# Moving the query and key blocks of an encoder step's projection from the RWKV preparation to behind five iterations of its state chain

## The chip, the cores and the metric

The kernel runs on one core of one Trainium2 chip. The metric is the device time of one execution in microseconds (us); lower is better. The medians are taken over several executions of the same program; a profiled execution of the same program gives the rows that are read below.

## What is computed

One inference step of a one-layer streaming encoder, in float32, on 1024 prompt tokens and 8 sample streams with 16 new tokens each (1152 tokens, 9 tiles of 128, width 1024):

```
x = x + 0.5 * SwiGLU_1(RMSNorm(x))
P = RMSNorm(x) @ w_in                 # RWKV columns: r, k, v (512 each) and 256 low-rank; then q, k, v (512 each)
mix = concat(RWKV7(P_rwkv), BandAttn(P_att)) @ w_out
x = x + mix
x = x + 0.5 * SwiGLU_2(RMSNorm(x))
y = RMSNorm_final(x)
```

RWKV7 keeps a 64 x 64 state for each of 8 heads and carries it through the tokens one after the other: decay, removal along a normed key direction, addition of a key-value product, then a read by the query, a group norm and a gate. BandAttn is softmax attention of 8 heads over a band of 512 + 64 earlier positions with a relative bias; the streams use their caches. The outputs are y, the last projected rows, the states and the new key and value rows.

## The kernel before

The weights and the activations of a projection are split into a float32r part and a rest, and a product is made in three passes (`_mm_cols`, L211 to L220): 8 chunks of the inner dimension times 3 passes, for each of 3 groups of 384 tokens, so 72 matmuls for a column block of 128. `_load_w` (L159) loads a block's weights over the SP queue into `raw`, and ScalarE and GpSimd split them into `spl`; in the middle part there are 2 `raw` and 3 `spl` buffers (L1141).

The first feed-forward half and the last one, each a long run of dense matmuls, lie before and behind the part that the change touches. That part goes as follows.

**Projection and preparation** (`_project`, L282). `shifted(c)` projects one RWKV column block (`ps_p`) into a buffer `pt` behind the row before it. There are 4 `pt` buffers. For each of 4 head pairs p, three blocks are projected (r, k, v), and `_rwkv_prepare` (L480) makes what the state chain needs for the pair, in 5 groups of 256 tokens and three stages: token shift, decays and key norms (`_prepare_tokens`, reads `pt` at L273 and L274), scaled keys and queries (`_prepare_chunks`), and products, transposes and gates, which go to DRAM over the SP queue (`_prepare_products`). Most of its operations are small ones on VectorE, ScalarE and GpSimd, with a few matmuls between them. Behind each pair L337 places two blocks of `_attention_in` (L396): the queries and the keys of that attention head pair. Such a block has 72 matmuls (`ps_qk`, 3 x 24), its evictions on ScalarE (L414) and VectorE (L415, L421), for keys a transpose (`ps_ko`, L429) and its eviction (L432), one weight load on the SP queue and 7 (queries) or 10 (keys) stores on ScalarE's queue. Behind pairs 1 and 2 and behind the whole, `_invert` (L665) inverts the chunks' triangular matrices on VectorE, 62 operations a call, four calls.

**Chain and values.** `_rwkv` (L860) is a generator of 10 iterations of 4 chunks each; `_rwkv_run` (L752) makes one. A chunk is a sequence in which every step needs the one before: 16 matmuls (L771), a copy on VectorE, 16 matmuls (L776), four copies, 16 matmuls (L780), two multiplications on VectorE, beside 16 matmuls for the output (L784). An iteration has 192 matmuls that write `ps_c`. Its operands are loaded one iteration ahead over the SP queue (`_rwkv_load`, two buffers each), and the group norm of an iteration (`_rwkv_post`, L823) runs inside the next one, partly on GpSimd. L1153 places three iterations, then `_attention_inputs` (L355): the blocks of `QK[NQK:]` (none, as `NQK` is 8), the key caches, and the values, 18 tiles of 24 matmuls with 256 columns (`ps_av`, 432 in all).

**Attention.** Only then are the projection's pools closed and attention's buffers opened in their place (L1156, L1164). `_attention` (L1008) yields 74 steps for 72 units (pair, tile, head): scores (`ps_s`, L941), exponentials, transposes (`ps_pt`, L980, 256 in all), products with the values (`ps_o`, L994). Its loads are issued on GpSimd's queue (`k.aq`, L1167). L1169 to L1171 place one chain iteration and six units by turns, then the rest of the units. The output projection comes behind all of it.

**What sets the order.** No order is written out by hand. A scheduler at build time goes through the operations with the program order as priority and its own estimate of their durations: on each engine it places the earliest operation whose operands and buffers are ready, and when that one isn't ready, a later one that is. So matmuls that need nothing from the preparation or the chain end up in their gaps, as far as buffers allow. The order that comes out is fixed in each engine's queue, and a queue is worked off in order.

```
QK = [(p, kind) for p in range(NPAIR) for kind in range(2)]   # L55
NQK = 8                                                       # L56
...
        for q in QK[NQK * p // NPAIR:NQK * (p + 1) // NPAIR]: # L337
            _attention_in(k, w, *q)
```

Of the kernel before, what the change touches and what calls it, by code (L numbers as in the profile page):

```python
# [19 lines left out]
NPT = 8                 # prompt token tiles  # L20
NT = 9                  # token tiles, the last one holds the sample group
T = NT * P
TG = 384                # tokens of a moving operand
DFF = 2816
NF = DFF // P
NB, NQ = 8, 16          # sample streams and their new tokens
HD = 64
NPAIR = 4               # head pairs of each mixer
NH = 2 * NPAIR
NRC = 14                # 128-wide column chunks of the RWKV part of w_in  # L30
L = 32                  # RWKV chunk
NG = 5                  # groups of 8 RWKV chunks, the last one is the sample group
NCK = 8 * NG            # RWKV chunks of a head
# [4 lines left out]
# rows of the table of small vectors  # L38
# [8 lines left out]
# ---------------------------------------------------------------- constants  # L47
# [8 lines left out]
NQK = 8  # L56
# [18 lines left out]
def _vectors(k, parts, queue):  # L75
    """Columns of the table of small vectors."""
# [29 lines left out]
def _bias_tables(k, a):  # L106
    """Per head pair, in DRAM: the relative biases of a prompt tile's two near key tiles and of
    the sample group's keys, less the table's first entry (the bias of all far keys), with the
    masks added."""
# [16 lines left out]
    for p in range(NPAIR):  # L126
# [10 lines left out]
        # row q, column c of the skewed view: entry 127 + c - q  # L137
# [14 lines left out]
# ---------------------------------------------------------------- weights, norms  # L152
# [6 lines left out]
def _load_w(k, src, shape, rearr, **kw):  # L159
    """A weight block of 1024 words a partition as its float32r part and the rest."""  # L160
    raw = k.w.tile([P] + shape, F32, tag="raw", bufs=k.nraw, name="raw")
    k.wq.dma_start(raw, src.rearrange(rearr, **kw) if rearr else src)
    pool, nspl = k.spl
    d = pool.tile([P, 2] + shape, F32R, tag="spl", bufs=nspl, name="spl")
    _split(k, d, raw)
    return d
# [6 lines left out]
def _rms(k, i, xn):  # L173
    """The inverse root mean square of token tile i; xn is scratch."""
# [13 lines left out]
def _norm_t(k, v0):  # L188
    """By steps: k.xg[g] <- split of the transposed, normed token group g."""
# [21 lines left out]
def _mm_cols(k, ps, w, g):  # L211
    """ps [128 columns, 384 tokens] <- w^T x of token group g, in three passes."""
# [10 lines left out]
# ---------------------------------------------------------------- SwiGLU  # L223
# [44 lines left out]
# ---------------------------------------------------------------- projection  # L268

def _shift_mix(k, out, cur, prev, c):  # L270
    """out <- prev mu + cur (1 - mu) for column chunk c."""
# [5 lines left out]
def _sample_view(t):  # L277
    """The sample columns of a shifted chunk: [stream, shifted-in row and new tokens]."""
    return t[:, 1025:SPAN].rearrange("p (b l) -> p b l", l=NQ + 1)


def _project(k, a):  # L282
# [5 lines left out]
    # token-shift states, transposed to [column, stream, chunk]  # L288
# [8 lines left out]
    def shifted(c):  # L297
        """Column chunk c of the projection behind the row before: prompt, then the streams."""
# [18 lines left out]
    # the low-rank inputs: the gate's sigmoid, and tanh(decay part) | rate part  # L317
# [37 lines left out]
def _attention_inputs(k, a):  # L355
    """Queries and keys, then values, to DRAM and the caches."""
# [8 lines left out]
    # attention values, token-major  # L365
# [30 lines left out]
def _attention_in(k, w, p, kind):  # L396
    """Queries (scaled, kind 0) or keys of attention head pair p, feature-major and split, to
    DRAM; the keys also go to the caches, token-major."""
# [7 lines left out]
    # part, head, feature  # L406
# [33 lines left out]
# ---------------------------------------------------------------- RWKV  # L440

def _prepare_constants(k, a):
# [5 lines left out]
    # masks of the products: strict s < t for the keys, s <= t for the queries  # L448
# [22 lines left out]
    # the decays' and the rates' low-rank weights, each over zeros for the other's inputs  # L471
# [8 lines left out]
def _rwkv_prepare(k, p, low, pr, pk, pv):  # L480
    """What the chunks of head pair p need besides the running state, to DRAM, in three stages a
    group; a group's stage comes after the stage before of the next group."""
# [6 lines left out]
def _prepare_more(k):  # L489
    """The later stages of the groups that are begun."""  # L490
# [11 lines left out]
def _prepare_tokens(k, p, g, low, pr, pk, pv):  # L502
    """Token shift, decays and the norms of the key directions."""
# [3 lines left out]
    q = _K()  # L507
# [10 lines left out]
    # token shift of r, k, v  # L518
# [15 lines left out]
    # decay: running sum of the sigmoids inside a chunk, and its exponentials  # L534
# [17 lines left out]
    # key direction, normed inside the head  # L552
# [11 lines left out]
def _prepare_chunks(k, q):  # L564
    """The scaled keys and queries of the chunks."""
# [20 lines left out]
    # keys and queries scaled by the decay since the chunk's start  # L586
# [17 lines left out]
def _prepare_products(k, q):  # L604
    """Products of keys with keys and queries inside the chunks, masked; the time-major keys and
    values, the gates and the offsets."""
# [27 lines left out]
    # time-major keys  # L634
# [7 lines left out]
    # time-major values  # L642
# [7 lines left out]
    # gates with the group norm's weight; its offset and the values' bonus, gated  # L650
# [14 lines left out]
def _invert(k, *parts):  # L665
    """To DRAM: (I - A)^-1 by substitution, an inverse a partition, of every chunk of the parts: a
    head pair and its groups."""
# [20 lines left out]
def _chunk_constants(k, a):  # L688
# [5 lines left out]
    # state weights: the identity over the chunk's keys  # L694
# [6 lines left out]
def _rwkv_load(k, i):  # L701
    """The operands of four chunks, half i % 2 of group i // 2.

    Of every chunk and head, by turns:
# [532 lines left out]
```

## Time and profile before

| | us |
|---|---|
| median of 3 runs | 2640.08 |
| lowest and highest run | 2636.32, 2643.09 |
| span of the profiled execution (first to last instruction) | 2638.9 |

The profiled execution is told by its span alone; what lies around the span has no row. The span is 1.2 us under the median of the runs, so a change of the span is added to the median as it is.

In the profile a row of a stretch gives, for a window of the span, the busy time of each engine in it with the number of its instructions, the granted TensorE clock as a share of full speed, the share of time in which the DMA engines were busy and the rate. A busy TensorE is not one at its peak: the ends of matmuls are modelled, so the times of neighbours overlap, and the spacing of starts tells more than the durations. The profile cuts the part that the change touches at these points: 943.5, where the first pair's projection is done; 1029.4, 1120.4 and 1211.4, the same for the other three pairs; 1292.9, the chain's first matmul; 1357.8, the end of the values; 1386.9, the first scores; 1607.0, the chain's end; 1685.5, the end of attention.

### The profile page before, as it was taken

Reading aid. Unit: us, or ns where it says so; the run is one execution under the profiler, and the core shown is the slowest. Engines: PE = TensorE matmul, PEld = TensorE weight load, DVE = VectorE, ACT = ScalarE, POOL = GpSimd, SP = SyncE. Lnnn points to the kernel's source line nnn. Section 1 sums busy time; section 2 is a strip of 40 time slices with the busy share of each in tenths; the row PEclk is TensorE's granted clock in tenths of the full one; section 3 lists DMA queues with packets and bytes.
Section 4 is the critical chain, followed back from the end, with each engine's and each line's share of the span. In section 5 each row is a group of like instructions: output and inputs, shape, how many; then the busy total and the mean of one; then the engine's idle time right before and its main releaser. Section 6 shows DMA issues by size and latency. Waiting matters only on the chain.

```text
span 2638.9 us, 39574 instructions
## 1 busy us (share of the span) xinstructions
PE 2534.1 (96%) x16344; PEld 2296.9 (87%) x16344; DVE 1206.3 (46%) x2460; ACT 646.9 (25%) x1294; POOL 762.5 (29%) x686
## 2 busy tenths in 40 slices
PE   8999999999999899999987898899999999999998
PEld 8999999999998799989865666689999999999997
DVE  4442344234426344585846766523442344234425
ACT  5111111111111444344113334504111111111112
POOL 3222222222221334344133423103222222222231
PEclk9999999999999899999987789899999999999999
DMA  5311111111111243354669856301111111111111
GB/s 185 113 41 40 40 49 40 41 40 49 41 32 72 65 135 114 113 165 143 171 155 234 198 122 183 123 0 57 48 40 41 40 49 41 41 40 49 40 32 73
DMA packets 247797, 217.39 MB, mean 82 GB/s; under 512 B 54016, under 2 KB 218496, under 8 KB 247232
## 3 DMA queue, kind: packets, MB, share of 16 engines
q1 hardware_dynamic: 214252, 167.74, 21.9%
q0 software_dynamic: 7648, 25.43, 4.0%
q10 hardware_dynamic: 25716, 21.68, 2.7%
q8 instruction: 129, 2.11, 0.3%
q14 instruction: 52, 0.43, 0.1%
HBM read 155.35 MB, written 59.45 MB: 81 GB/s over the span
## 4 chain that ended last, share of the span: by engine, by line
PE 49%; DVE 5%; issue 2%; DMA 1%; POOL 1%; SPq 1%; ACT 1%; POOLq 0%; ACTq 0%; DVEq 0%
PE pg L220 3%; PE pg L218 3%; PE pg L219 3%; PE pu L220 3%; PE pd L256 3%; PE pu L218 3%; PE pu L219 3%; PE pd L258 3%; PE pd L257 3%; PE ps_o L994 2%; PE ps_wo L1067 1%; PE ps_wo L1065 1%; PE ps_wo L1066 1%; PE ps_s L941 1%; PE ps_pt L980 1%
## 5 line engine op out<-in xcount | busy, mean ns | idle before, releaser
L156 POOL TENSOR_TENSOR spl<-raw,spl 128x1024 fp32r<-128x1024 f32 x166 | 399.4, 2407 | 794.0 <-ACT spl L155 793.9
L260 DVE TENSOR_TENSOR x<-pd,x 128x512 f32<-128x512 f32 x774 | 527.4, 691 | 7.0 <-PE pd L258 2.9
L244 DVE SCALAR_TENSOR_TENSOR hf<-pu,sl 128x384 f32<-128x384 f32 x132 | 73.6, 558 | 963.5 <-PE pu L220 948.4
L218 PE MATMUL pg<-xg,spl 128*128 128x384 f32 x1056 | 356.2, 337 | 0.0
L220 PE MATMUL pg<-xg,spl 128*128 128x384 f32 x1056 | 355.4, 337 | 0.0
L219 PE MATMUL pg<-xg,spl 128*128 128x384 f32 x1056 | 355.3, 336 | 0.0
L220 PE MATMUL pu<-xg,spl 128*128 128x384 f32 x1056 | 355.0, 336 | 0.0
L218 PE MATMUL pu<-xg,spl 128*128 128x384 f32 x1056 | 354.9, 336 | 0.0
L219 PE MATMUL pu<-xg,spl 128*128 128x384 f32 x1056 | 354.9, 336 | 0.0
L155 ACT ACTIVATE spl<-raw 128x1024 fp32r<-128x1024 f32 x166 | 174.9, 1057 | 634.6 <-PE pd L258 421.8
L256 PE MATMUL pd<-spl,h 128*128 128x512 f32 x792 | 310.6, 392 | 0.0
L258 PE MATMUL pd<-spl,h 128*128 128x512 f32 x792 | 310.4, 392 | 0.0
L257 PE MATMUL pd<-spl,h 128*128 128x512 f32 x792 | 310.4, 392 | 0.0
L247 POOL TENSOR_TENSOR h<-hf,h 128x384 fp32r<-128x384 f32 x132 | 133.9, 1014 | 591.0 <-ACT h L246 577.3
L218 PEld LDWEIGHTS pg<-xg,spl 128*128 128x128 f32 x1056 | 198.5, 188 | 1.7
L219 PEld LDWEIGHTS pg<-xg,spl 128*128 128x128 f32 x1056 | 198.5, 188 | 1.5
L220 PEld LDWEIGHTS pg<-xg,spl 128*128 128x128 f32 x1056 | 198.3, 188 | 0.0
L220 PEld LDWEIGHTS pu<-xg,spl 128*128 128x128 f32 x1056 | 198.2, 188 | 0.0
L218 PEld LDWEIGHTS pu<-xg,spl 128*128 128x128 f32 x1056 | 198.2, 188 | 0.0
L219 PEld LDWEIGHTS pu<-xg,spl 128*128 128x128 f32 x1056 | 198.2, 188 | 0.0
L258 PEld LDWEIGHTS pd<-spl,h 128*128 128x128 f32 x792 | 148.6, 188 | 33.7
L257 PEld LDWEIGHTS pd<-spl,h 128*128 128x128 f32 x792 | 148.5, 188 | 31.9
(227 smaller groups left out, 3710.3 us busy)
## 6 DMA issues: line engine op xcount, KB each, us to landing
raw<-in_w_ff_gate_dram SPq DMA_DIRECT2D x44, 512.0 KB
raw<-in_w_ff_up_dram SPq DMA_DIRECT2D x44, 512.0 KB
raw<-in_w_ff_down_dram SPq DMA_DIRECT2D x44, 512.0 KB
raw<-in_w_in_dram SPq DMA_DIRECT2D x26, 512.0 KB
q<-qk POOLq DMA_DIRECT2D x24, 384.0 KB, 7.4
ard<-ar SPq DMA_DIRECT2D x20, 256.0 KB
grd<-gram SPq DMA_DIRECT2D x20, 256.0 KB
wsd<-tb SPq DMA_DIRECT2D x20, 256.0 KB
```

Source lines behind the costliest of these rows:

```text
L155: k.nc.scalar.activation(dst[:, 0], raw, AF.Copy)
L156: k.nc.gpsimd.tensor_tensor(dst[:, 1], raw, dst[:, 0].bitcast(F32), ALU.subtract)
L218: mm(ps, w[:, 0, c], hi[:, c], start=c == 0, stop=False)
L219: mm(ps, w[:, 0, c], lo[:, c], start=False, stop=False)
L220: mm(ps, w[:, 1, c], hi[:, c], start=False, stop=c == KC - 1)
L244: nc.vector.scalar_tensor_tensor(hf, pu[:, :TG], 0.5, sl, ALU.mult, ALU.mult)
L247: nc.gpsimd.tensor_tensor(h[:, 1, s], hf, h[:, 0, s].bitcast(F32), ALU.subtract)
L256: mm(ps, ph[:, 0, a], pd[:, 0, b], start=j == 0, stop=False)
L257: mm(ps, ph[:, 0, a], pd[:, 1, b], start=False, stop=False)
L258: mm(ps, ph[:, 1, a], pd[:, 0, b], start=False, stop=j == len(pend) - 1)
L260: nc.vector.tensor_tensor(xs, ps, xs, ALU.add)
L994: mm(po[hs, :P], q.v[:, u.j0 + j, hs], u.pt[:, j * P:(j + 1) * P], start=j == 0, stop=j == nj - 1)
```

## The change

`NQK` becomes 0, so the loop at L337 places no block, and all eight blocks of queries and keys are placed by `_attention_inputs`, pair by pair, ahead of the values. Five chain iterations instead of three are placed ahead of `_attention_inputs`, and eight units instead of six behind each of the five iterations that are left. No operation, buffer or queue is added or removed. (The diff also strips comments and docstrings, with no effect.)

```diff
-NQK = 8
+NQK = 0
...
         chain = _rwkv(k, a)
-        for _ in range(3):
+        for _ in range(5):
             next(chain)
         _attention_inputs(k, a)
         s_xg.close()
...
             for _ in chain:
-                for _ in range(6):
+                for _ in range(8):
                     next(units, None)
```

## Rows read from the trace of the kernel before

**Rows 1.** the profile's page: span, TensorE's busy time, granted clock in 40 slices

```profile
span 2638.9 us, 39574 instructions
PE 2534.1 (96%) x16344; PEld 2296.9 (87%) x16344; DVE 1206.3 (46%) x2460; ACT 646.9 (25%) x1294; POOL 762.5 (29%) x686
PEclk9999999999999899999987789899999999999999
```

**Rows 2.** busy time in seven stretches: PE, PEld, DVE, ACT, POOL; granted clock; DMA

```profile
943.50:1029.40 85.90, 83.58 (x589) 79.72 (x588) 39.11 (x99) 38.87 (x89) 34.32 (x50) 1.00 0.39 124
1029.40:1120.40 91.00, 86.80 (x624) 82.00 (x624) 58.20 (x159) 36.38 (x83) 37.03 (x49) 0.98 0.44 134
1211.40:1292.90 81.50, 74.66 (x645) 69.28 (x647) 66.81 (x175) 29.83 (x72) 28.42 (x39) 0.98 0.63 184
1292.90:1357.80 64.90, 63.27 (x881) 49.18 (x881) 41.15 (x118) 8.43 (x23) 11.75 (x9) 1.00 0.61 144
1357.80:1386.90 29.10, 16.45 (x271) 11.26 (x263) 13.46 (x38) 1.95 (x6) 11.00 (x15) 0.55 0.82 185
1386.90:1607.00 220.10, 195.55 (x2436) 139.22 (x2436) 153.91 (x432) 78.69 (x223) 85.02 (x103) 0.81 0.82 183
1607.00:1685.50 78.50, 68.62 (x564) 54.26 (x565) 49.59 (x139) 41.00 (x118) 14.22 (x20) 0.91 0.40 115
```

**Rows 3.** the query and key blocks alone, second of four preparations, columns PE, PEld, DVE, ACT

```profile
1029.40:1120.40 91.00, 31.05 (x144) 26.13 (x144) 4.76 (x9) 2.93 (x6) 0.98 0.44 134
```

**Rows 4.** timeline of PE, dense projection and value matmuls: start, duration, line

```profile
939.72 0.33 PE L220 MATMUL ps_p<-xg,spl 128*128 128x384 f32 x1
...
943.36 0.33 PE L220 MATMUL ps_p<-xg,spl 128*128 128x384 f32 x1
...
1347.79 0.28 PE L379 MATMUL ps_av<-spl,xg 128*128 128x256 f32 x1
...
1348.86 0.28 PE L379 MATMUL ps_av<-spl,xg 128*128 128x256 f32 x1
```

**Rows 5.** TensorE's waits in the first three preparations: total, times, longest

```profile
PE ps_ko L429 <- DVE qk L421: 4.6, 2, 2.4
```

**Rows 6.** the inversions' operations alone, second preparation

```profile
1029.40:1120.40 91.00, 23.66 (x62) 0.98 0.44 134
```

**Rows 7.** timeline of DVE, second preparation: last reads and next use of pt

```profile
1051.92 0.34 DVE L274 SCALAR_TENSOR_TENSOR mix<-pt,omu,mix 128x128 f32<-128x128 f32 x1
...
1053.14 0.72 DVE L303 COPY pt<-stt 128x8 f32<-128x8 f32 x2
```

**Rows 8.** the values alone, stretch from the chain's start

```profile
1292.90:1357.80 64.90, 43.17 (x238) 31.47 (x237) 3.91 (x11) 1.00 0.61 144
```

**Rows 9.** the chain's matmuls into ps_c, three stretches

```profile
1292.90:1357.80 64.90, 15.66 (x480) 10.89 (x480) 22.09 (x69) 1.00 0.61 144
1357.80:1386.90 29.10, 9.26 (x192) 6.75 (x192) 9.94 (x30) 0.55 0.82 185
1386.90:1607.00 220.10, 49.69 (x1248) 35.54 (x1248) 58.80 (x181) 0.81 0.82 183
```

**Rows 10.** timeline of POOL about the end of the values

```profile
1357.15 0.85 POOL L890 DMA_DIRECT2D q<-qk  x1 [1.94 <-PE ps_av L379]
1370.80 1.25 POOL L853 TENSOR_TENSOR yo<-yo,gb 128x512 f32<-128x512 f32 x1 [12.80 <-DVE yo L851]
...
1376.57 0.59 POOL L896 DMA_DIRECT2D kt<-qk  x1
```

**Rows 11.** timeline of PE: the first scores

```profile
1386.88 0.66 PE L941 MATMUL ps_s<-kt,q 128*128 128x128 f32 x2 [6.29 <-DMA kt<-qk]
```

**Rows 12.** attention's transposes, two stretches

```profile
1386.90:1607.00 220.10, 34.07 (x148) 19.65 (x148) 24.28 (x60) 0.81 0.82 183
1607.00:1685.50 78.50, 20.19 (x108) 12.93 (x108) 17.39 (x44) 0.91 0.40 115
```

**Rows 13.** the SP queue's own waits, 1200 to 1680

```profile
SPq L725 <- PE ps_yc L784: 55.4, 7, 15.3
```

## The prediction, made before the changed kernel was run

> **What bounds the kernel now.** I read the profile's page first: TensorE is busy for 96% of the span [rows 1], so the limit is TensorE, or the moments in which it has too little to do. The slices of the granted clock say where those are: full speed nearly everywhere, and 7 to 9 tenths in slices 20 to 26, about 1320 to 1715 us. The change lies in the stretch 943.5 to 1685.5, so I cut that into its stages and asked for each engine's busy time [rows 2]. In the preparations (943.5 to 1211.4; the third, not shown, is 91.0 us like the second) TensorE is busy for 86.80 of 91.00 us at a clock of 0.98; no other engine comes near. From the chain's first matmul to the end of the values it is busy for 63.27 of 64.90 us at 1.00. Then come 29.10 us with 16.45 busy at 0.55, and 220.10 us of chain and attention at 0.81. So the preparations and the start of the chain are bound by TensorE's work, and time is lost in the gap and in the mixed stretch. In a stretch that is full, moving matmuls only moves time; a gain must come from the last two, a loss from preparations that are no longer full.
>
> **1. The blocks leave the preparations.** Dense matmuls of 384 columns start every 3.64/21 = 0.1733 us, those of the values every 1.07/9 = 0.119 us [rows 4]. A block has 72 matmuls, 12.5 us. Each preparation holds 144 of them [rows 3], two blocks. The first three lose 6 blocks, 75.0 us, and with them two waits for the keys' eviction, 4.6 us [rows 5]; VectorE loses 4.76 and ScalarE 2.93 us a preparation [rows 3]. What covers the preparation's gaps now? The next pair's first block: there are four `pt` buffers and three in use. The other two blocks need `pt` to be free. VectorE last reads it at 1051.92 and writes the next at 1053.14 [rows 7], 23 us behind the start at 1029.4. One block of 12.5 us for those 23 us, in which the preparation's own matmuls take about half, is nearly enough, and behind them 25 us are at hand. Bounds for what stays uncovered: below, nothing; above, all 25 us of each pair. I take 3 us a pair, 9 in all, near the lower end, because the second preparation is already full with fillers and waits for little but those keys. Together: 267.9 - 75.0 - 4.6 + 9.0 = 197.3 us, 65.8 a pair; the part shrinks by 70.6.
>
> **2. Fourth preparation to the chain's start.** 81.50 us [rows 2]. There is no next pair, so fillers are at hand as before. Before, they are two blocks (25.0 us) and 432 - 238 = 194 value matmuls [rows 8], 23.1 us; after, 48.1 us of query and key blocks. The chain waits for VectorE's inversions there; I leave 81.5. The third inversion may reach into this preparation, since the cycles are shorter, but TensorE has filler for that time, so it costs nothing.
>
> **3. Chain beside the fillers.** An iteration writes `ps_c` with 192 matmuls. In 64.90 us there are 480, 2.5 iterations [rows 9], beside 238 value matmuls of 28.3 us [rows 8], so an iteration costs (64.9 - 28.3)/2.5 = 14.6 us of a full TensorE. Afterwards the fillers are 8 blocks (99.8) and all values (51.4) less 48.1, 103.1 us, and five iterations cost 73.0: 176.1 us instead of 64.9, +111.2. With parts 1 and 2 the values end 40.6 us later, with 5 iterations done and not 2.5. Of this 36.6 is the price of the 2.5 iterations.
>
> The moved stores go with their blocks: 68 on ScalarE's queue and 8 weight loads on SP's, past the chain's loads. ScalarE is busy for 8.43 of 64.90 us there, and DMA for 0.61 of the time [rows 2], with 0.82 borne in the next rows; I cost them at nothing. If that cover fails, the SP queue is where: it waits for the chain's buffers up to 15.3 us at a time [rows 13], and weights queued behind would come late; but three `spl` buffers hold over 25 us of filler.
>
> **4. The gap.** Attention's first scores start 29.1 us behind the values and wait for keys [rows 11]. The loads are issued on GpSimd, and behind the first of them the queue stands 12.80 us for the chain's group norm; keys are issued at 1376.57 [rows 10]. Afterwards some 30 us of fillers are left when the fifth iteration is done (103.1 us of fillers go into five iterations of 26 us, of which 14.6 is the chain's), so the chain stands ready and that norm is met sooner. Bounds: 0 and the 12.8 us plus what was queued behind; I take -10. In 19 us the chain makes some 0.9 iterations alone (1.0 in 29.1 before [rows 9], with a wait for its own loads).
>
> **5. Chain beside attention.** Before, 1248/192 = 6.5 iterations are left, afterwards 5 - 0.9 = 4.1. Without the chain, 108 transposes take 78.5 us [rows 12], 0.727 each with all that belongs to them; the 148 of the mixed stretch are 107.6 us, so an iteration costs (220.1 - 107.6)/6.5 = 17.3 us there, more than in part 3 as the clock is 0.81. Bounds for one taken away: 14.6 (part 3) and 29.1 (one alone in the gap). I take 17.3, the stretch's own: -41.5. Eight units for six behind an iteration only sort the same steps.
>
> **Sum**: +40.6 - 10 - 41.5 = -10.9. The profiled span is 2638.9, 1.2 under the median of the runs, so 2640.1 - 10.9, **2629 us**. What a measurement of this kernel can tell from no change is about 0.3%, 8 us.
>
> **Rivals.** *No gain.* An iteration taken out of the mixed stretch saves just what it costs before, 14.6 us, and the gap stays 29.1 with its iteration: +40.6 - 36.5 = +4, 2644 us. For it: GpSimd's queue may stand again, and what slows the mixed stretch may be attention's own loads (DMA busy 0.82). Against it: the clock, 1.00 there and 0.81 here. Chance 0.24.
>
> *VectorE sets the pace of the preparations (slower).* The matmuls gone, a pair can't be faster than its chain of small operations. In the second preparation VectorE works 58.2 us, 23.66 of it inversions [rows 6]; without the blocks' evictions 53.4. My 65.8 us a pair asks for a share of 81%. The fourth shows 66.81 of 81.50, 82%; the second only 64%. The forecast turns slower by over 8 us from 72 us a pair (65.8 + 18.9/3), a share of 74%. Priced at 70%: 76.3 us, 3 x 10.5 = +31, 2660 us. Chance 0.20.
>
> *The clock falls in the preparations (slower).* With little to do TensorE went at 0.55 in the gap [rows 2]. If it did so for the 23 us of each of three preparations, each would lose 23 x 0.45 = 10 us: +31, 2660 us. Chance 0.05, since a ready block stands in those 23 us. The Trainium skill, "TensorE: Matmul & The Clock Gate", Part 1: The HAM clock gate, speaks against the change here: an idle array drops to half its clock and must work again to get it back. By that rule it would be this rival's sum, without it mine; the gap's row agrees with the rule.
>
> *The blocks stay where they were.* They need nothing of the chain, so the scheduler may put them into the preparations again. Against it: the three `spl` buffers then hold the next pair's weights, which come first. Part 1 would be no change: 36.6 - 10 - 41.5 = -15, 2625 us. Chance 0.05.
>
> **Chances and range.** The forecast has 0.46; by the 14.6 to 29.1 us of part 5 and 0 to 12.8 of part 4 its own range is 2612 to 2643, and about a sixth of it lies within 8 us of no change. Faster: 0.38 + 0.05 = 0.43. Within 0.3%: 0.08 from it, 0.22 from no gain, 0.30. Slower: 0.20 + 0.05 + 0.02 from no gain's upper edge, 0.27. The range reaches from 2608 to 2656, which leaves out the dearer half of the two slower rivals and the best of the forecast.
>
> **What would show it.** The fourth pair's projection ending near 1141 instead of 1211.4, with TensorE over 90% busy in three preparations of 66 us; the chain's first matmul near 1222; no `ps_qk` before 1141; the values' end near 1398 with five iterations done, the first scores near 1417, attention's end near 1675. Preparations of 72 us or more, or a clock under 0.9 in them, prove the slower rivals right; a mixed stretch that shortens by no more than 36 us for 2.4 iterations fewer proves the first. I am wrong in kind if the chain is slowed beside the blocks, so that the values are done before its fifth iteration.

## The result, and the profile after

The changed kernel takes 2661.47 us (median of 4, 2654.24 to 2662.54), the kernel before, run beside it, 2641.59 (2636.32 to 2643.69): a ratio of 1.0076 with an interval of 1.0059 to 1.0094, so it is slower by some 20 us. The forecast was 2629, the range ended at 2656. The profiled execution has a span of 2660.0 us for 2638.9. The page's lines that answer to [rows 1]:

```profile
span 2660.0 us, 39639 instructions
PE 2547.9 (96%) x16344; PEld 2295.5 (86%) x16344; DVE 1203.3 (45%) x2460; ACT 645.9 (24%) x1294; POOL 763.3 (29%) x686
PEclk9999999999999899988998898899999999999999
```

The share of TensorE is the same and VectorE does the same work. What differs is where the clock dips: slices 17 and 18, counted from 0 (about 1130 to 1265 us), which were full before, and a shallower dip in slices 20 to 25. To see it by stage I cut both traces at the same marks: the end of the fourth pair's projection, the chain's second step (the first matmuls of L776), the end of the values, the first scores, the chain's end and attention's end. The chain's first matmuls (L771) no longer serve as a mark, as they now stand 19.5 us ahead of the second step (1226.92 and 1246.43; before 1292.85 and 1294.53). Six windows of the changed kernel, with the columns of [rows 2]:

```profile
943.50:1137.60 194.10, 179.26 (x1336) 164.73 (x1334) 134.75 (x351) 89.29 (x211) 86.89 (x131) 0.97 0.37 115
1137.60:1246.40 108.80, 88.84 (x644) 80.92 (x643) 84.99 (x223) 35.04 (x82) 37.23 (x50) 0.87 0.62 178
1246.40:1439.00 192.60, 185.10 (x2090) 144.69 (x2089) 86.50 (x237) 29.49 (x67) 37.92 (x25) 0.96 0.57 146
1439.00:1462.80 23.80, 15.35 (x280) 10.41 (x278) 12.10 (x35) 5.36 (x9) 10.22 (x13) 0.61 0.77 220
1462.80:1611.80 149.00, 134.92 (x1620) 98.26 (x1620) 105.68 (x306) 62.38 (x184) 67.22 (x86) 0.88 0.83 187
1611.80:1705.70 93.90, 84.14 (x646) 65.38 (x647) 57.32 (x164) 48.40 (x139) 18.90 (x27) 0.84 0.44 124
```

The first three stages of the kernel before, cut at the same marks:

```profile
943.50:1211.10 267.60, 256.83 (x1829) 243.44 (x1828) 159.26 (x416) 111.39 (x252) 107.22 (x147) 0.99 0.43 132
1211.10:1294.50 83.40, 76.13 (x663) 70.45 (x662) 68.30 (x180) 29.91 (x72) 28.42 (x39) 0.98 0.63 183
1294.50:1356.60 62.10, 60.91 (x830) 47.41 (x830) 39.37 (x112) 7.96 (x21) 11.11 (x8) 1.00 0.61 143
```

The chain's matmuls in the third to fifth stage of the changed kernel, as in [rows 9]:

```profile
1246.40:1439.00 192.60, 33.55 (x992) 23.64 (x992) 47.73 (x146) 0.96 0.57 146
1439.00:1462.80 23.80, 9.25 (x208) 6.62 (x208) 9.44 (x29) 0.61 0.77 220
1462.80:1611.80 149.00, 25.78 (x690) 17.99 (x690) 33.09 (x102) 0.88 0.83 187
```

The same marks in all profiled executions (us; "its" are chain iterations inside the third stage, its `ps_c` matmuls over 192; the last column is the median of the runs, and the ratio to the kernel before run beside it):

| kernel | 3 preparations | to 2nd step | chain + fillers (its) | gap | mixed | attention alone | median, ratio |
|---|---|---|---|---|---|---|---|
| before | 267.6 | 83.4 | 62.1 (2.33) | 30.3 | 218.9 | 79.4 | 2641.59 |
| after | 194.1 | 108.8 | 192.6 (5.17) | 23.8 | 149.0 | 93.9 | 2661.47, 1.0076 |
| blocks alone | 194.5 | 105.4 | 160.3 (3.25) | 25.8 | 197.6 | 83.9 | 2669.23, 1.0126 |
| counts alone | 267.0 | 82.0 | 62.1 (2.33) | 30.0 | 203.3 | 93.9 | 2642.53, 1.0024 |
| after, short inversions | 185.7 | 86.3 | 190.8 (5.25) | 26.3 | 148.4 | 89.1 | 2628.07, 0.9967 |
| before, short inversions | 260.1 | 81.6 | 58.4 (2.33) | 29.2 | 209.7 | 81.7 | 2618.62, 0.9935 |
| after, three calls | 193.4 | 96.0 | 205.3 (5.25) | 26.9 | 149.0 | 88.8 | 2656.77, 1.0071 |
| before, three calls | 260.0 | 89.5 | 52.6 (1.75) | 26.1 | 226.3 | 74.9 | 2630.74, 0.9965 |
| after, values first | 194.0 | 93.3 | 188.2 (5.33) | 33.4 | 158.2 | 85.8 | 2655.90, 1.0067 |
| after, evictions on ScalarE | 195.2 | 92.7 | 205.8 (5.33) | 23.8 | 164.8 | 89.1 | 2670.98, 1.0135 |
| after, late fourth call | 196.3 | 106.3 | 185.8 (5.17) | 23.9 | 148.5 | 93.8 | 2649.24, 1.0046 |
| before, late fourth call | 268.1 | 83.4 | 64.8 (2.58) | 30.0 | 216.0 | 80.9 | 2641.74, 1.0009 |
| after, three calls, late | 192.8 | 95.6 | 198.5 (5.25) | 26.0 | 151.8 | 91.6 | 2651.84, 1.0052 |
| after, copy on ScalarE | 194.4 | 100.2 | 196.7 (5.22) | 24.8 | 151.1 | 90.6 | 2656.15, 1.0070 |
| after, values first, late | 196.0 | 93.2 | 190.9 (5.42) | 32.8 | 154.6 | 91.8 | 2656.88, 1.0076 |
| before, three calls, late | 261.7 | 89.3 | 59.9 (2.25) | 37.6 | 209.2 | 81.1 | 2636.65, 0.9993 |
| before, three calls, copy on ScalarE | 263.7 | 93.1 | 53.2 (1.83) | 25.3 | 217.3 | 78.6 | 2637.81, 0.9997 |
| half the blocks | 224.6 | 95.3 | 131.0 (3.92) | 21.7 | 178.7 | 82.3 | 2632.72, 0.9977 |
| half, late | 225.5 | 94.5 | 140.1 (3.92) | 21.7 | 178.2 | 80.9 | 2639.83, 1.0000 |
| half, late, keys early | 229.8 | 86.9 | 130.0 (3.92) | 21.2 | 169.6 | 81.9 | 2620.70, 0.9929 |

After against before, by stage: -73.5, +25.4, +130.5, -6.5, -69.9, +14.5, together +20.5. The largest surprise is the second number: a stretch that I had left unchanged. TensorE's waits in it (total, times, longest):

```profile
PE ps_ko L429 <- DVE qk L421: 6.4, 2, 4.5
PE ps_l L348 <- DVE inv_t L681: 6.2, 1, 6.2
PE ps_g L624 <- DVE kb L598: 4.1, 2, 3.2
PE ps_k L557 <- ACT sq L554: 3.0, 2, 2.6
PE ps_t L637 <- DVE gram L626: 0.2, 1, 0.2
```

All but those of `ps_k` are for VectorE. In the same stretch of the kernel before the waits are `ps_g` 3.8, `ps_ko` 2.7 and `ps_gl` 0.3, 6.8 us in all. Two of the changed kernel's in TensorE's timeline:

```profile
1145.87 0.45 PE L348 MATMUL ps_l<-ident,last 128*126 128x128 f32 x1 [6.16 <-DVE inv_t L681]
...
1242.41 0.44 PE L429 MATMUL ps_ko<-ident,qk 128*128 128x128 f32 x2 [4.46 <-DVE qk L421]
...
1243.48 0.52 PE L218 MATMUL ps_qk<-xg,spl 128*128 128x384 f32 x1
1243.80 0.52 PE L219 MATMUL ps_qk<-xg,spl 128*128 128x384 f32 x1
...
1246.43 0.43 PE L776 MATMUL ps_c<-wx,tt 32*32 32x64 f32 x16
```

The first is a lone transpose of the projection's last rows. It needs a VectorE copy (L314) that stands in VectorE's queue among the inversion's last operations, and TensorE's queue stands with it though block matmuls that need nothing of either are next (1145.96). Behind the second, block matmuls take 0.52 us and start every 0.32, where they take 0.33 and start every 0.173 at full speed [rows 4]: the lower of the clock's two levels. What VectorE does at the first of these (its timeline: the third inversion's first operation, the copy, the inversion's last operation, and the fourth pair's next mixing behind it):

```profile
1115.56 0.67 DVE L681 TENSOR_TENSOR inv_t<-inv_w,inv_a 112x31 f32<-112x31 f32 x1
...
1145.56 0.16 DVE L314 COPY last<-pt 128x8 f32<-128x8 f32 x1
...
1147.94 0.21 DVE L683 TENSOR_TENSOR inv_w<-inv_w,inv_t 112x31 f32<-112x31 f32 x1
...
1153.92 1.27 DVE L274 SCALAR_TENSOR_TENSOR mix<-pt,omu,mix 128x256 f32<-128x256 f32 x3
```

The projection ends at 1137.6 and the third inversion (the one behind pair 2, with 112 rows) at 1148.2; the fourth pair's mixing, done for its first group at 1134.8, goes on only at 1153.9. Its last mixing (L274) begins 39.2 us behind the projection, 22.9 in the kernel before. The call that the chain's start needs begins at 1193.0, its result is stored and loaded again (SP queue)

```profile
1233.67 0.31 SPq L685 DMA_DIRECT2D inv<-inv_w  x1
...
1236.23 0.34 SPq L715 DMA_DIRECT2D tt<-inv  x1
```

and the chain's second step follows at 1246.43. The same points before are 1244.2, 1284.0, 1287.5 and 1294.5. So of the 73.5 us that the projection is ahead, 51 are left where that call begins, 48 at the second step, and 43 at the chain's second iteration (1322.3 before, 1279.0 after).

### The profile page after: what moved, and what is told of

It reads as the page before. It is cut to its first block, busy times and chain, and to the rows that moved or that the text cites. A ratio compares the mean times of both kernels' runs of the same rounds, so it can differ in the third digit from the quotient of the medians.

```text
span 2660.0 us, 39639 instructions
## 1 busy us (share of the span) xinstructions
PE 2547.9 (96%) x16344; PEld 2295.5 (86%) x16344; DVE 1203.3 (45%) x2460; ACT 645.9 (24%) x1294; POOL 763.3 (29%) x686
## 4 chain that ended last, share of the span: by engine, by line
PE 49%; DVE 2%; DMA 2%; ACT 1%; issue 1%; POOL 0%; SPq 0%; POOLq 0%; ACTq 0%; DVEq 0%
PE pg L218 3%; PE pg L220 3%; PE pg L219 3%; PE pu L218 3%; PE pd L256 3%; PE pu L220 3%; PE pu L219 3%; PE pd L258 3%; PE pd L257 3%; PE ps_o L994 2%; PE ps_s L941 1%; PE ps_wo L1067 1%; PE ps_wo L1065 1%; PE ps_wo L1066 1%; PE ps_yc L784 1%; PE ps_pt L980 1%
## 5 line engine op out<-in xcount | busy, mean ns | idle before, releaser
L156 POOL TENSOR_TENSOR spl<-raw,spl 128x1024 fp32r<-128x1024 f32 x166 | 401.5, 2420 | 848.2 <-ACT spl L155 820.5
```

The source lines that it names most:

```text
L156: k.nc.gpsimd.tensor_tensor(dst[:, 1], raw, dst[:, 0].bitcast(F32), ALU.subtract)
```

## The experiments

The theory to begin with, A: the third inversion falls into the fourth preparation, where VectorE's line of work then sets the pace, and TensorE, whose queue is worked off in order, stands for it and loses clock. The rivals: B, the chain's iterations are dearer beside query and key blocks, as the blocks' evictions stand in VectorE's queue among the chain's copies; C, the new counts (5 and 8) cost the time.

**The change taken apart.** First the blocks alone, with the counts left at 3 and 6:

```diff
-NQK = 8
+NQK = 0
```

> The blocks move as in the changed kernel, the chain keeps three iterations ahead of them and six units behind each later one. Theory A (the loss lies between the fourth preparation and the chain's start: the third inversion now falls into that preparation and TensorE's queue stands for VectorE): still about 20 us over the kernel before, 2655 to 2668, as nothing of that stretch is undone. Theory B (the chain beside query and key blocks is dearer, as they bring evictions on VectorE): less of the loss, 2648 to 2658, since two iterations fewer lie beside the blocks. Theory C (the counts 5 and 8 are what costs): within 8 us of the kernel before.

Then the counts alone, with `NQK` left at 8:

```diff
-        for _ in range(3):
+        for _ in range(5):
             next(chain)
...
-                for _ in range(6):
+                for _ in range(8):
```

> The blocks stay in the preparations; five iterations are placed ahead of the values and eight units behind each of the other five. Theory A: within 8 us of the kernel before, the chain starting at 1293 as there. Theory B: the same. Theory C: 2652 or more.

Measured: 2669.23 for the blocks (1.0109 to 1.0143), 2642.53 for the counts (1.0009 to 1.0040). C falls: the blocks alone are 32 us slower than the kernel before (just above the 2655 to 2668 that A expected), the whole change 20, and the counts alone do nearly nothing, since the values end with 2.33 iterations done whatever the count allows. Only where more filler is left do two more iterations fit beside it.

**Inversions cut short.** 4 of the 31 steps, in both kernels.

```diff
-    for s in range(L - 1):
+    for s in range(4):
```

> The changed kernel with 4 of the 31 substitution steps of each inversion; the other 27 are left out of the computation, which takes some 80 us of VectorE's work away. Theory A: the stretch from the fourth pair's projection to the chain's start shrinks from some 107 us to 75 or less, TensorE no longer stands there, and the kernel is no slower than the next run, which leaves the same steps out of the kernel before. Theory B: it stays 10 us or more above the next run.

> The kernel before with 4 of the 31 substitution steps of each inversion, the other 27 left out of the computation. All theories: the chain starts earlier, by up to the two inversions of 24 us that follow the last preparation less what fillers TensorE has still to do; 2615 to 2640. It is the reference for the run before it.

Measured 2628.07 and 2618.62. By the ratios the changed kernel gains 29 us (1.0076 to 0.9967) and the kernel before 17, and the distance between them falls from 20 to 9.5. The windows of the second and third stage of the changed kernel with short inversions:

```profile
1129.20:1215.50 86.30, 77.35 (x635) 70.33 (x634) 49.70 (x125) 35.14 (x82) 32.95 (x48) 0.98 0.68 203
1215.50:1406.30 190.80, 182.81 (x2115) 143.07 (x2115) 73.94 (x206) 29.40 (x68) 37.81 (x25) 0.99 0.60 154
```

108.8 us become 86.3 and the clock rises from 0.87 to 0.98, with nearly the same fillers (266 block matmuls for 276): most of what was lost there was lost to the inversions. Which of the four calls it was, this edit doesn't tell, as it cuts them all. A also expected 75 us or less for the stretch and the changed kernel level with the other; 9.5 us were left, close to the 10 or more that B expected. Nor is all of the delay the inversions': with them cut short the last mixing still begins 30.6 us behind the projection and the third call 46.0, for 39.2 and 55.4 in the changed kernel and 22.9 and 33.1 in the kernel before. So of the 22.3 us by which that call comes later, 12.9 have another cause, which no run here names.

**Where the inversions stand.** Three calls of up to 128 rows instead of four do the same work, with none behind pair 2, so that none runs while the fourth pair is prepared.

```diff
-            _invert(k, (0, 0, NG))
+            _invert(k, (0, 0, NG), (1, 0, 3))
-        elif p == 2:
-            _invert(k, (1, 0, NG), (2, 0, 2))
...
-        _invert(k, (3, 0, 2))
-        _invert(k, (2, 2, NG), (3, 2, NG))
+        _invert(k, (2, 0, 2), (3, 0, 2))
+        _invert(k, (1, 3, NG), (2, 2, NG), (3, 2, NG))
```

> The changed kernel with three calls of the inversion instead of four, nothing left out: behind pair 1 one call takes pair 0 and the first three groups of pair 1, there is no call behind pair 2, and the two calls behind the preparations share the rest. So no inversion runs in the fourth preparation, and VectorE is spared one call (62 operations, some 24 us). Theory A (the third inversion falls into the fourth preparation, and TensorE's queue stands for VectorE): fourth preparation to the chain's start goes from 108.8 us back to 80 to 88, and the time to 2630 to 2645 us where the changed kernel has 2661. Theory B (the chain is dearer beside query and key blocks, 17 us an iteration for 14.6): the stretch beside the fillers stays at 185 to 193 us. If A is wrong (what costs there are the blocks' own evictions), that stretch stays above 100 us and the time above 2652.

> The kernel before with the same three calls, nothing left out. Its third inversion runs in the fourth preparation as well, beside fillers that need VectorE little. Theory A: it gains less than the changed kernel does by the same edit, 0 to 10 us (2627 to 2638), so that the change costs 3 to 12 us instead of 20. If the inversion costs both kernels alike (A wrong), it gains as much as the changed kernel does, within 4 us.

2656.77 and 2630.74. The expectation for the changed kernel failed: the second stage fell by 12.8 us, to 96.0 (80 to 88 expected), but the third grew by 12.7, at a clock of 0.94. By the ratios the changed kernel gains 1 us and the kernel before 9, the reverse of what A expected of the two. With the three calls in both, the second stages lie 6.5 us apart (96.0 and 89.5) and not 25.4, which fits A for that stage, but the whole times lie 26 us apart and not 20. The second and third stage of the changed kernel with three calls:

```profile
1136.90:1232.90 96.00, 80.79 (x630) 74.31 (x628) 76.01 (x198) 34.29 (x80) 34.14 (x48) 0.91 0.67 191
1232.90:1438.20 205.30, 190.51 (x2119) 148.80 (x2119) 87.73 (x242) 30.07 (x69) 37.82 (x25) 0.94 0.55 141
```

The chain's first iteration took 56 us there (1215.9 to 1272.2), 52 in the changed kernel, 29.5 before and 26 with short inversions: it runs beside the last call. So A was too narrow, and became A2: VectorE's whole line, the rest of the preparations and two inversions, sets when the chain gets going. So the last call was placed behind the chain's third iteration in program order, alone in both kernels, and with the three calls in both:

```diff
-        _invert(k, (2, 2, NG), (3, 2, NG))
...
         for _ in range(3):
             next(chain)
+        _invert(k, (2, 2, NG), (3, 2, NG))
```

> The changed kernel with the fourth call of the inversion (the chunks from the third group on of pairs 2 and 3) placed behind the chain's third iteration instead of ahead of the chain; nothing left out. In the changed kernel the chain's first iteration takes 52 us (1226.9 to 1279.0) while that call runs on VectorE until 1271; with inversions cut short it took 26. Theory A2 (VectorE's line of work, the rest of the preparations and two inversions behind one another, sets when the chain gets going, and TensorE's queue stands for it): the first iteration takes 26 to 35 us, the second begins 12 to 25 us earlier behind the fourth pair's projection than the changed kernel's 141.4 us, and the time falls by 8 to 20 us, to 2641 to 2653. Rival (the call only moves, and the chain's later iterations pay for it, as the waits did when the third call was taken out): the second iteration comes earlier, but fillers still end 295 to 302 us behind the projection, and the time stays at 2655 to 2663.

> The kernel before with the same call placed behind its three iterations. There the first iteration takes 29.5 us, 3 more than with short inversions, so little is to be had: theory A2 expects 2632 to 2642, and a gap to the changed kernel with the same edit of 0 to 12 us. If the edit gains as much here as there, the place of the call is not what tells the two kernels apart.

> The changed kernel with three calls instead of four and the last of them behind the chain's third iteration. Theory A2: both things that hold VectorE up are gone, so that the projection's end to the chain's second iteration takes 105 to 118 us (141.4 in the changed kernel, 111.2 in the kernel before, 109.8 with short inversions), and the time is 2632 to 2645. The rival (later iterations pay) expects 2650 to 2660.

> The kernel before with three calls and the last of them behind its three iterations: the first candidate for a kernel better than both. The three calls alone gave 2630.7 for 2640.4. A2 expects another 0 to 6 us, 2624 to 2634. If the last call then comes too late for the group that needs it (the fifth iteration), the mixed stretch gets longer and the time is above 2636.

2649.24 (1.0027 to 1.0064) and 2641.74 (0.9999 to 1.0019): 12 us for the changed kernel by the medians and 8 by the ratios, whose intervals still touch (1.0059 to 1.0094 without the edit), and none for the other, as A2 had it. The first iteration took 42.7 us, more than the 26 to 35 expected. In VectorE's queue the call did not go behind the chain: it runs from 91.5 to 140.2 us behind the projection, for 94.0 to 133.4 without the edit, and 50 of its 62 operations still lie beside the first iteration. But the third stage ran at full clock:

```profile
1139.80:1246.10 106.30, 86.33 (x648) 78.65 (x646) 85.03 (x223) 35.01 (x82) 37.17 (x50) 0.90 0.65 184
1246.10:1431.90 185.80, 179.30 (x2090) 140.57 (x2089) 87.69 (x237) 29.54 (x67) 37.91 (x25) 1.00 0.60 150
```

Both edits together, 2651.84, give no more than the second alone, and miss the 2632 to 2645 expected. On the kernel before, three calls gained 10 us alone, and 3 and nothing in two kernels that hold them with another edit (2636.65 here, 2637.81 below), so that gain isn't sure.

**What the fillers need of VectorE.** Four kernels spare VectorE while the inversions run. The values, which ScalarE evicts, come ahead of the blocks (the lines of L361 to L363 behind the loop of the values), without and with the late call; the blocks' two VectorE evictions go to ScalarE; or the keys' copy alone does, in a fifth kernel also on the kernel before with three calls. The copy's edit:

```diff
-        nc.vector.tensor_scalar(raw, ps[:, :TG], scale, None, ALU.mult)
+        nc.scalar.activation(raw, ps[:, :TG], AF.Copy, scale=scale)
```

> The changed kernel with the values placed ahead of the query and key blocks, the same operations. The values' evictions are on ScalarE, so fillers that need nothing of VectorE stand beside the inversions, and all eight blocks stand beside the chain. Theory A: fourth preparation to the chain's start falls from 108.8 us to 85 to 95, as the keys' transposes no longer stand there for VectorE. Theory B: the stretch of chain and fillers gets dearer than the 17.2 us an iteration of the changed kernel, 18 us or more, as more blocks lie beside it. Without B it is 17 or less. The time: by A alone 2645 to 2652 us, with B as well 2652 to 2662. Against A, if the inversion itself is too long for any filler: the first stretch stays over 102 us.

> The changed kernel with the values ahead of the blocks and the last inversion behind the chain's third iteration, nothing left out. Singly these gave 5 and 12 us. If the rest of the loss is the fillers' need of VectorE beside the inversions, the two add up: 2640 to 2646, level with the kernel before. If the blocks cost their surplus wherever the chain runs beside them, the first is given back: 2648 to 2655.

> The changed kernel with the blocks' two evictions of VectorE on ScalarE: the copy for the caches, and the low part, which becomes a plain scaled copy there, so that the low parts of queries and keys hold the whole value instead of the rest. The number of operations stays. Theory A, by its narrow reading (TensorE stands since the keys' copy waits behind the inversion): fourth preparation to the chain's start falls from 108.8 to 90 to 100 us. Theory B (the blocks' evictions on VectorE hold up the chain's copies): an iteration beside the fillers costs 14.6 to 15.5 us instead of 17.2, and the stretch of 192.6 us shrinks by 8 to 13. Both together: 2640 to 2650 us. If neither evictions nor the copy matter, the time stays at 2658 to 2664, and what is dear beside the blocks is something else (the preparation's own waits for the inversion, and the lower clock behind them).

> The changed kernel with the scaled copy that the keys' transposes read made by ScalarE instead of VectorE; nothing left out. It removes the one wait of TensorE for the keys' copy that stands next to the chain's start (4.5 us, and half clock behind it). If that wait is what is left of the loss: the stretch from the projection's end to the chain's second step falls from 108.8 to 96 to 102 us and the time by 6 to 10 us, to 2650 to 2655. If the third inversion's end sets the chain's start anyway, and TensorE only waits elsewhere: less than 4 us, 2657 to 2662.

> The kernel before with three calls of the inversion instead of four (2630.7 beside 2640.4 in an earlier run) and the keys' copy on ScalarE: a candidate for the best version. In its preparations TensorE waits for that copy some 4.6 us, which would go: 2624 to 2630. If other work of TensorE's queue takes the wait's place, it stays at 2629 to 2633.

Measured, in this order: 2655.90, 2656.88, 2670.98, 2656.15 and 2637.81. Only the first lies in its expectation, where that allowed for B. Each of the first four shortens the second stage, by 15.5, 15.6, 16.1 and 8.6 us, and gives about half of it or more back, so that no ratio is clear of the changed kernel's on the better side: with the values first in the gap and the mixed stretch (+9.6 and +9.2), with the evictions on ScalarE in the third stage (+13.2) and the mixed one (+15.8). The last stays level with the kernel before. B is not borne out: without the blocks' two evictions on VectorE the stage with the chain is no cheaper (205.8 us, though ScalarE then carries them), and with all eight blocks beside the chain an iteration takes (188.2 - 102.7) / 5.33 = 16.0 us besides its fillers, where B expected 18 or more.

Why an iteration looks dearer there can be read off the third stages. TensorE's busy time by the clock, less the fillers (0.1733 us a block matmul, 0.119 a value matmul [rows 4]), over the iterations: before (60.91 x 1.00 - 27.6) / 2.33 = 14.3 us; after (185.10 x 0.96 - 103.6) / 5.17 = 14.4; short inversions (182.81 x 0.99 - 105.2) / 5.25 = 14.4; three calls (190.51 x 0.94 - 105.5) / 5.25 = 14.0; late call (179.30 x 1.00 - 103.6) / 5.17 = 14.6. Over all twenty traces this estimate gives 13.6 to 14.7. So by it the iteration's own price is the same beside blocks and values. What is added is TensorE's idle time and lost clock: 7.5 and 7.4 us in the changed kernel's third stage, 1.2 and none before.

**Half the change.** One block behind each pair, four later, counts 4 and 7; then with the late call as well; then with the keys as the early blocks, too.

```diff
-NQK = 0
+NQK = 4
...
-QK = [(p, kind) for p in range(NPAIR) for kind in range(2)]
+QK = [(p, kind) for kind in (1, 0) for p in range(NPAIR)]
```

> Half the change: one query or key block behind each of the four pairs, the other four placed by the second part, four iterations ahead of it and seven units behind an iteration. The first three preparations hold three blocks instead of six, so they should take 267.6 less 37.5 and one wait, 228 us, 76 a pair. Theory A2 with a threshold: a pair's line of small operations needs some 70 us (the changed kernel's three took 194 us and left 16 us more of the pair's mixing behind the projection than before), so at 76 nothing falls behind: the last mixing of the fourth pair ends 23 to 26 us behind its projection (22.9 before, 39.2 in the changed kernel), the projection's end to the chain's second iteration takes 111 to 118 us, and the time is 2636 to 2646. If it is a matter of degree, half of everything: 31 us, 126 us and 2648 to 2655.

> Half the change (a block behind each pair, four by the second part) with the last inversion behind the chain's third iteration, nothing left out. The first iteration of the chain took 45.9 us in half the change, 18 us of it while the last inversion runs on VectorE. Theory A2: 30 to 40 us, and 4 to 10 us less in all, 2622 to 2629. If the place of that inversion matters only where all blocks stand beside the chain: 2630 to 2636.

> The same with the four key blocks behind the pairs and the four query blocks behind the chain's iterations. Queries have no transposes that wait for VectorE's copy, so the 5.7 us of TensorE's waits for it in the stretch before the chain go, and so does the copy beside the inversions. Theory A2: 3 to 8 us less than the run before, 2616 to 2626. If the waits only move into the preparations (keys' transposes there, 2.3 us a block): equal within 3 us.

Half the change takes 2632.72 (0.9964 to 0.9991), better than both ends, though neither reading of its expectation had that: its stages lie between (the fourth pair's last mixing begins 35.6 us behind the projection, the second iteration 127.3). Pair by pair that distance of the mixing is 25.2, 30.4, 30.6, 35.6 us; 25.1, 31.0, 35.3, 39.2 in the whole change; 25.1, 31.0, 30.8, 30.6 there with short inversions; 25.1 and three times 22.9 before. So a step of some 8 us is there already with half the blocks gone, and with short inversions too; only what comes on top of it in the whole change, some 4 us a pair, goes away with them. The late call costs the half 7 us (2639.83, outside both expectations), and the third stage's clock falls to 0.94; why it hurts here and helps the whole change is open. With the keys early as well it is **2620.70, a ratio of 0.9929 (0.9917 to 0.9942)**, the best of all that leave nothing out, and 19 us less than the run before where 3 to 8 were expected. The second and third stage without the keys early, the first three with them, and TensorE's waits in the second, without and with:

```profile
1169.00:1263.50 94.50, 80.07 (x636) 71.76 (x636) 73.66 (x192) 35.38 (x82) 36.42 (x50) 0.95 0.67 193
1263.50:1403.60 140.10, 132.70 (x1557) 104.84 (x1557) 69.53 (x190) 18.96 (x47) 25.85 (x18) 0.94 0.58 149
```

```profile
943.50:1173.30 229.80, 219.27 (x1568) 201.66 (x1567) 146.62 (x390) 99.29 (x229) 94.12 (x135) 0.99 0.41 124
1173.30:1260.20 86.90, 80.43 (x654) 72.54 (x653) 71.96 (x187) 34.95 (x81) 35.63 (x50) 1.00 0.69 206
1260.20:1390.20 130.00, 124.50 (x1526) 98.62 (x1526) 69.12 (x190) 18.04 (x44) 25.84 (x18) 0.96 0.65 158
```

```profile
PE ps_g L624 <- DVE kb L598: 7.5, 6, 4.3
PE ps_ko L429 <- DVE qk L421: 5.9, 3, 3.9
...
```

```profile
PE ps_g L624 <- DVE kb L598: 3.5, 6, 1.3
...
PE ps_ko L429 <- DVE qk L421: 0.2, 1, 0.2
...
```

With queries for fillers, which have no transposes that wait for VectorE, 13.9 us of waits become 6.3, and the clock stays at 1.00 through the second stage. In the preparations up to 1160 no wait for the keys' copy shows. The second stage accounts for 7.6 of the 19 us; the third gives 10.1 and the mixed stretch 8.6, the preparations take 4.3 back, and what shortens the later two no run isolates. Keys early without the late call, and with all eight blocks placed otherwise, weren't run.

## Why the prediction was wrong

**Part 1 was right.** The preparations shrank by 73.5 us, 70.6 predicted, to 64.7 a pair at a clock of 0.97; the projection ended at 1137.6, 1141 predicted, and no block stood in them. What it left out is that the end of a projection is not the end of its pair's work. VectorE did 134.75 us in them; before it was 159.26, of which 14.3 were the blocks' evictions, so 10 us of its other work, 7.0 of them inversion, slid behind the mark. The reading that the preparation "waits for little but those keys" left out TensorE's nine waits for VectorE's `kb`, 5.2 us in the three preparations for the keys' 4.6; afterwards these were 11.3 us, and the next stage paid more.

**Part 2 failed, and with it the forecast.** "I leave 81.5 ... TensorE has filler for that time, so it costs nothing." It cost 25.4 us up to the chain's second step (7.6 up to its first matmuls, the prediction's mark: 89.3 for 81.8). The filler was there (276 block matmuls, 47.8 us, 48.1 predicted), but a matmul in an in-order queue that waits for VectorE holds up all filler behind it. Idle time rose from 7.3 to 20.0 us (window less busy time), and the lost clock, 1.5 us before (76.13 x 0.02), was 11.5 (88.84 x 0.13). With short inversions the surplus is 4.7 us, with half the change and the keys early 3.5. The 20 us windows with waits of 6.2, of 2.6, of 3.2 and 2.0, and of 4.5 us have a granted clock of 0.83, 0.83, 0.74 and 0.74, the two others 1.00. The Trainium skill, "TensorE: Matmul & The Clock Gate", Part 1: The HAM clock gate, says that an idle array falls to half its clock; the prediction weighed that for the preparations, and this trace agrees with it one stage later.

```profile
1140.00:1160.00 20.00, 14.13 (x94) 12.13 (x95) 14.22 (x40) 6.83 (x18) 7.48 (x14) 0.83 0.48 128
1160.00:1180.00 20.00, 18.38 (x159) 16.33 (x159) 16.30 (x41) 13.63 (x34) 11.30 (x20) 1.00 0.56 179
1180.00:1200.00 20.00, 17.37 (x135) 15.48 (x133) 11.92 (x35) 4.76 (x13) 9.21 (x15) 0.83 0.50 165
1200.00:1220.00 20.00, 14.91 (x92) 14.51 (x93) 16.51 (x38) 4.33 (x9) 6.23 (x2) 0.74 0.98 258
1220.00:1240.00 20.00, 17.95 (x117) 17.29 (x115) 18.69 (x56) 3.41 (x6) 2.39 (x1) 1.00 0.62 174
1240.00:1260.00 20.00, 15.51 (x123) 11.49 (x124) 16.12 (x39) 2.69 (x5) 2.35 (x1) 0.74 0.85 227
```

**Part 3 was undersized.** +111.2 predicted, +130.5 measured. 2.83 iterations came into the stage instead of 2.5 (4.8 us at 14.6); the rest is idle time and clock, not a price of the blocks. The values did end with five iterations done, as predicted, but at 1439 instead of 1398.

**Part 4 was near**: -6.5 for -10. **Part 5 was cautious**: mixed stretch and rest fell by 55.4 us for -41.5, 19.6 for each of the 2.82 iterations that left it (1248 less 706 `ps_c` matmuls) instead of 17.3. Without these 13.9 us the forecast would have missed by more. Its own range was added up too narrow: the bounds that it names, 14.6 to 29.1 us for 2.4 iterations and 0 to 12.8 for the gap, give 2598 to 2646 and not 2612 to 2643; the measured time lies outside both.

So the gains that were forecast came: 6.5 in the gap, and 13.5 from iterations that cost 14.8 beside fillers, (62.1 - 27.6) / 2.33, and 19.6 beside attention (55.4 less 2.83 x 14.8). The losses were 26 us in the second stage, where the fillers are worth 1.0 us less than before, and 13 in the third (130.5 less 76.0 of fillers and 2.83 x 14.8). Half the change has the same gains, 8.6 and 13.9 us by the same sums, with only 1.58 iterations moved, and of the losses 16 and 4: by these sums that is why it is faster.

**The rivals.** "VectorE sets the pace of the preparations" gave 2660 us and names the right engine, but not the place: I let it decide at 72 us a pair, and the pairs took 64.7. The line fell behind without slowing the projection, and the bill came in the next stage. That its 2660 lies next to the measured 2661 is luck. The no-gain rival's condition (the mixed stretch shortens by no more than 36 us) didn't come; the clock in the preparations held (0.97); the blocks didn't stay.

Shown is that the inversions cause most of the second stage's loss (25.4 us beside the kernel before, 4.7 with them cut short in both), and that keys standing as fillers beside them are a part of that stage's loss, though not that the whole time follows. Not settled are the 7.5 to 9.5 us that stay between the two kernels with short inversions or with the late call: by stage, with short inversions, they lie in the chain beside fillers, but no edit took them away alone.

## What to carry to other kernels

Filler hides another engine's work only as long as nothing in the same queue waits for that engine: before moving independent work next to a long stretch of another engine, look at what each piece needs of that engine, and put there the pieces that need nothing. When a stage gets shorter, follow each engine's last operation of the stage and not the mark of the busiest one, since a slower line falls behind and is paid for in the next stage. A move whose gain saturates and whose cost grows with the amount is worth trying by half.

## What was not expected of the hardware

An inversion's operation on VectorE takes 0.2 us at either end of a call and 0.4 in its middle, but some take 2.0 to 2.6. Each such one of the changed kernel between 1110 and 1280 us lies beside GpSimd's split of a weight block (L156), and ends 0.1 to 0.3 us behind it:

```profile
1126.86 0.41 DVE L681 TENSOR_TENSOR inv_t<-inv_w,inv_a 112x240 f32<-112x240 f32 x1
1127.30 2.49 DVE L683 TENSOR_TENSOR inv_w<-inv_w,inv_t 112x240 f32<-112x240 f32 x1
```

```profile
1126.90 2.63 POOL L156 TENSOR_TENSOR spl<-raw,spl 128x1024 fp32r<-128x1024 f32 x1 [7.06 <-ACT spl L155]
```

The Trainium skill, "SBUF — State Buffer", SBUF: two separate sides, says that VectorE operations with two SBUF inputs and GpSimd operations that read SBUF exclude each other for a whole instruction; the trace agrees. Five were held up so, 9.6 us over 0.4 each. The best version has five as well (9.9 us between 1135 and 1293), so this doesn't tell the kernels apart, but it lengthened the inversions that weights were split beside.
